# Stick-breaking attention from running products of sigmoid(-z), with differenced values shifted through DRAM

## The chip, the cores and the metric

The kernel runs on one core of a Trainium2 chip. The metric is the device time of one execution in microseconds (us); lower is better. The engines are named as in the profile: PE multiplies matrices (PEld loads its weights), DVE is the vector engine, ACT the scalar engine, POOL is GpSimd, and SP issues most of the loads.

## The reference, cut to what matters

One layer of an encoder on 1024 tokens of width 1024: two token mixers side by side (causal pooling and stick-breaking attention), gated, projected and added to the input; then an MLP with squared ReLU. The part that the change rewrites is the attention, eight heads of 64 channels:

```python
z = einsum('bhqd,bhkd->bhqk', qb, kb) * scale
mask = arange(t1)[None, :] < arange(t0, t1)[:, None]        # s < t
log_1mb = where(mask, log_sigmoid(-z), 0.0)
tail = cumsum(log_1mb, reverse=True) - log_1mb
attn = where(mask, exp(log_sigmoid(z) + tail), 0.0)
out = einsum('bhqk,bhkd->bhqd', attn, vb)
```

So A[t,s] = sigmoid(z[t,s]) times the product of sigmoid(-z[t,j]) over s < j < t. Write F[t,s] for the product of sigmoid(-z[t,j]) over s <= j < t. Then F[t,t] = 1 and A[t,s] = F[t,s+1] - F[t,s], since sigmoid(z) = 1 - sigmoid(-z).

## The kernel before

All activations are held transposed or in tiles of 128 tokens. Every float32 product of weights and activations is made as three matmuls in a reduced float32 format on high and low parts (`mm3`, L113 to L117). The kernel has four phases: `phase_in` (norm, pooling mixer, first q and k), `phase_attention`, `phase_post` (branch and output projections) and `phase_mlp`.

In `phase_attention` the rows of scores of one head go from row tile 7 to row tile 0. `att_scores` makes z in PSUM with two matmuls for each chunk of at most 512 columns (L561, L564), then two sigmoids on ACT: F = sigmoid(-z) (L565) and T = sigmoid(z) (L566). POOL sets T to zero at and above the diagonal of the last 128 columns (`affine_select`, L568), DVE turns F into a running product from right to left (`tensor_tensor_scan`, L574; its second operand `past` forces 1 where s >= t), and DVE multiplies T by F one column further right (L578). T is then A.

`att_steps` takes a group g of four row tiles: for each source tile s it transposes the four blocks of T on PE (L591), splits them into a high part on ACT (L599) and a low part on DVE (L600), and one step later `att_products` multiplies by the v tile of s into the PSUM tile `o` (L616). A v tile holds, for four heads, 64 columns of high and 64 of low parts, so `o` has two halves by partition; after the last s they are copied and added into `oT` (L625, L627). `o` has one buffer. When s is the group's last tile, POOL clears part of the high and low tiles first (L597, L598).

Between these steps PE gets dense work as filler: gate projections (`job_gate`, stored through POOL's queue at L521), the q and k of later heads (`job_qk`) and v (`job_v`). `pump` counts out how many steps of filler stand between two steps of attention; with `pin`, the first matmul of each three is issued behind a mark that lies four marks back (L111 to L113). v of heads 0 to 3 is made at the start of head 0, source tiles 7 to 0, and v of heads 4 to 7 inside heads 3 and 4, tiles 0 to 7. `job_v` evicts one tile of 128 tokens by 256 columns with one ACT instruction (L508) and one DVE instruction (L509).

The order within each engine's queue is not that of the program: a planner sets it when the kernel is built, from its own estimates of durations, and `issue_after` adds an edge that it has to keep. Each engine then runs its queue strictly in that order and waits on semaphores.

POOL's queue also issues `weight_sums` (L1067, L1069): 32 transfers from DRAM to DRAM that prepare sums of MLP weights, some of them accumulating. Before the change one of them is issued after the masking of every second row (L673 to L675), 28 in the attention phase.

Of the kernel before, what the change touches and what calls it, by code (L numbers as in the profile page):

```python
# [19 lines left out]
F32 = mybir.dt.float32  # L20
F32R = mybir.dt.float32r
BF16 = mybir.dt.bfloat16
AF = mybir.ActivationFunctionType
ALU = mybir.AluOpType
# [28 lines left out]
class Block:  # L53
# [53 lines left out]
    def mm3(self, ps, terms, first=True, last=True):  # L107
        nc = self.nc
        n = len(terms)
        for i, (wh, wl, rh, rl) in enumerate(terms):  # L110
            if self.pin and len(self.marks) >= LAG:  # L111
                with self.tc.issue_after(self.marks[-LAG].ins):
                    nc.tensor.matmul(ps, wh, rh, start=first and i == 0, stop=False)  # L113
            else:
                nc.tensor.matmul(ps, wh, rh, start=first and i == 0, stop=False)  # L115
            nc.tensor.matmul(ps, wh, rl, start=False, stop=False)  # L116
            nc.tensor.matmul(ps, wl, rh, start=False, stop=last and i == n - 1)  # L117

    def dense_steps(self, ps, wt, rhs, c0=0, cn=H):

# [51 lines left out]
    def build(self):  # L172
# [61 lines left out]
        self.rp = tc.alloc_tile_pool(name="row", bufs=1, side="left")  # L234
        self.rb = [self.rp.tile([P, H], F32, name=f"rb{h}") for h in range(2)]
        self.rcol = cp.tile([P, NK], F32, name="rcol")
        edge = tc.alloc_tile_pool(name="edge", bufs=1, side="right")
        self.edge = edge.tile([P, 24], F32, name="edge")
        self.dps = tc.alloc_tile_pool(name="att_d", bufs=2, space=PSUM)
# [11 lines left out]
    def phase_in(self):  # L251
# [46 lines left out]
            load(1, k, 2)  # L298
        for t, src in zip((self.eye, self.rcnt), self.consts):
            nc.sync.dma_start(t, src)  # L300
        past = pa.tile([P, 1024], F32, name="past")
        nc.gpsimd.memset(past, 1.0)
        nc.gpsimd.affine_select(
# [112 lines left out]
        def pool_mix(g, cur):  # L416
            sc = self.vt[:, V_PSC + g : V_PSC + g + 1]
            yl = us[g]
            ph = pb.tile([P, 1024], F32R, name="ph")
            pq = pb.tile([P, 1024], F32R, name="pq")  # L420
            nc.scalar.copy(ph, cur)
            nc.vector.tensor_sub(pq, cur, ph.bitcast(F32))
            for h in range(2):
                c = slice(h * H, h * H + H)
                d = self.zps.tile([P, H], F32, name="dm", tag=("o", "at")[h], bufs=h + 1)
                self.mm3(d, [(wmh[:, g, :], wml[:, g, :], ph[:, c], pq[:, c])])
                nc.scalar.activation(cur[:, c].bitcast(F32R), d, AF.Copy, scale=sc)
                nc.vector.scalar_tensor_tensor(
                    out=yl[:, c].bitcast(F32R), in0=d, scalar=sc, in1=cur[:, c], op0=ALU.mult, op1=ALU.subtract
                )  # L430
            for t, scr in zip((cur, yl), self.yscr[g]):
                nc.gpsimd.dma_start(scr.bitcast(F32), t)
# [18 lines left out]
        pool_mix(2, pooled[2])  # L451
        pooled.append(pool_group(3))
        self.run(self.job_qk("k", 0, 0))
        pool_mix(3, pooled[3])
        self.run(self.job_qk("k", 0, 1))
        pb.release()

    def run(self, gen):
# [30 lines left out]
    def job_v(self, grp):  # L489
        nc = self.nc  # L490
        w = [self.weights(("v", grp, j), 1 - j) for j in range(2)]

        for t in range(NK) if grp else range(NK - 1, -1, -1):
            d = self.dps.tile([P, H], F32, name="dv", tag="d")
            h, c = t // 4, (t % 4) * P
            rh, rl = self.hT[h]
            for k in range(NK):
                wh, wl = w[k // 4]
                b = slice((k % 4) * 256, (k % 4) * 256 + 256)
                self.mm3(  # L500
                    d[:, :256], [(rh[:, k, c : c + P], rl[:, k, c : c + P], wh[:, b], wl[:, b])], k == 0, k == NK - 1
                )
                if k % 2:
                    yield
            v = self.vp.tile([P, 4, P], F32R, name=f"v{grp}_{t}", tag="v", bufs=9)
            dd = d[:, :256].rearrange("p (h x) -> p h x", h=4)
            r = self.rcol[:, t : t + 1]
            nc.scalar.activation(v[:, :, 0:64], dd, AF.Copy, scale=r)  # L508
            nc.vector.scalar_tensor_tensor(  # L509
                out=v[:, :, 64:128], in0=dd, scalar=r, in1=v[:, :, 0:64].bitcast(F32), op0=ALU.mult, op1=ALU.subtract  # L510
            )
            self.v[(grp, t)] = v

    def job_gate(self, i, h):
        nc = self.nc
# [22 lines left out]
    def att_scores(self, h, i):  # L538

        nc = self.nc
        p, j = h // 2, h % 2
        q, qs, k = self.qk[("q", p)][j], self.qk[("qs", p)][j], self.qk[("k", p)][j]
        w = (i + 1) * P
        tl = self.tp.tile([P, w], F32, name="T", tag=f"T{i}", bufs=1)
        f = self.tp.tile([P, 1024], F32, name="F", tag="F", bufs=1)
        tt = slice(i * P, i * P + P)  # L550
        past = self.past[:, 1024 - w :]

        low = min(H, w - 2 * P) if w > H else 0
        for c, n in ((low, w - low), (0, low)):
            if n == 0:
                continue
            top = c == low
            cols = slice(c, c + max(256, n))
            z = self.zps.tile([P, H], F32, name="z", tag="z", bufs=3)
            zz = z[:, : max(256, n)]  # L560
            m = nc.tensor.matmul(zz, q[:, tt], k[:, cols], start=True, stop=False)  # L561
            if top:
                self.marks.append(m)
            nc.tensor.matmul(zz, qs[:, tt], k[:, cols], start=False, stop=True)  # L564
            nc.scalar.activation(f[:, c : c + n], z[:, :n], AF.Sigmoid, scale=-1.0)  # L565
            nc.scalar.activation(tl[:, c : c + n], z[:, :n], AF.Sigmoid)  # L566
            if top:
                self.masked = nc.gpsimd.affine_select(  # L568
                    out=tl[:, w - P : w], in_=tl[:, w - P : w], pattern=[[-1, P]], compare_op=ALU.is_gt, fill=0.0,
                    base=0, channel_multiplier=1,  # L570
                )

            fr = f[:, c : c + n][:, ::-1]
            nc.vector.tensor_tensor_scan(  # L574
                fr, fr, past[:, c : c + n][:, ::-1], 1.0 if top else f[:, c + n : c + n + 1], ALU.mult, ALU.max
            )
            e = c + n - top
            nc.vector.tensor_mul(tl[:, c:e], tl[:, c:e], f[:, c + 1 : e + 1])  # L578
        return tl

    def att_steps(self, h, g, a):
# [3 lines left out]
        for s in range(4 * g + 4):  # L585
# [9 lines left out]
            c0, c = min(r0, 2) * P, r0 * P  # L595
            if r0 == 3:
                nc.gpsimd.memset(hi[:, c0:c].bitcast(F32), 0.0)  # L597
                nc.gpsimd.memset(lo[:, c0:c].bitcast(F32), 0.0)  # L598
            nc.scalar.copy(hi[:, c:], at[:, c:])  # L599
            nc.vector.tensor_sub(lo[:, c:], at[:, c:], hi[:, c:].bitcast(F32))  # L600
            self.att_products()
            self.pending = (h, g, s, o, hi, lo, c0)
            yield

    def att_products(self):
# [14 lines left out]
        if not last:  # L620
            return
        b = 64 * (h % 2)
        for c in (0, 256):
            u = self.sp.tile([P, 256], F32, name="ou", tag="ou", bufs=1)
            nc.scalar.copy(u[64:128, :], o[64:128, c : c + 256])  # L625
            at = slice(g * H + c, g * H + c + 256)
            nc.vector.tensor_add(self.oT[h // 2][b : b + 64, at], o[0:64, c : c + 256], u[64:128, :])  # L627

    def pump(self, share):
        self.credit += share  # L630
# [14 lines left out]

    def phase_attention(self):
        tc, nc = self.tc, self.nc
        self.oT = [self.op.tile([P, 1024], F32, name=f"oT{p}", tag=f"oT{p}") for p in range(4)]
        kw = dict(side="right", reuse_waits="tile")
        self.tp = tc.alloc_tile_pool(name="att", bufs=1, **kw)  # L650
        self.sp = tc.alloc_tile_pool(name="att_s", bufs=1, **kw)
# [6 lines left out]
        for h in range(8):  # L658
# [4 lines left out]
            self.queue = fl  # L663
            share = [WS[i] for i in ROWS] if h else [0.0] * 4 + [WS[i] for i in ROWS[4:]]
            w_in = max(0.0, n - (8 if h == 0 else 12) * self.w_out) / sum(share)
            vg = self.job_v(0) if h == 0 else None
            a = {}
            for n_row, i in enumerate(ROWS):
                if n_row == 4:
                    out = self.att_steps(h, 1, [a[r] for r in range(4, 8)])  # L670
                a[i] = self.att_scores(h, i)
                self.pump(w_in * share[n_row])
                if h < 7 and n_row % 2:  # L673
                    with tc.issue_after(self.masked.ins):
                        next(self.wsums)  # L675
                if h == 0 and n_row < 4:
                    if n_row == 0:
                        vq = [(vg, 32)] + [(f[0], f[1]) for f in self.fillers(-1)]
                    left = 12 if n_row < 3 else 999
                    while vq and left:  # L680
                        left -= 1
                        if next(vq[0][0], self) is self:
                            vq.pop(0)
                if out is not None:
                    for _ in range(2 if n_row > 3 else 1):
                        next(out, None)
# [705 lines left out]
```

## Time and profile before

| | us |
|---|---|
| median of 3 runs | 1275.92 |
| lowest, highest run | 1275.71, 1277.13 |
| span of the profiled execution | 1274.1 |

The span goes from the first to the last instruction of one profiled execution; the page gives no other time of that execution. The median of the runs is 1.8 us above it. Busy shares of an engine are shares of that span; "idle before" in a group of instructions is the time in which that engine stood just before them, followed by the line that ended it.

### The profile page before, as it was taken

What the parts mean: (1) busy time and instruction counts of PE and PEld (TensorE: products, weight loads), DVE (VectorE), ACT (ScalarE), POOL (GpSimd) and SP (SyncE); (2) the same over time, 40 slices, a digit from 0 to 9 for tenths busy, and PEclk for the clock granted to TensorE, in tenths of its full rate; (3) what the DMA queues carried; (4) which work ended last, traced back from release to release, by engine and by line L of the source; (5) the groups of instructions that cost most, each with busy time, mean ns of one, the idle gap of its engine ahead of it and who ended that gap; (6) DMA issues with size and microseconds to landing.
All of it is one profiled execution on the core that took longest, in us unless ns stands there. A gap on an engine that the chain in (4) does not pass through costs nothing.

```text
span 1274.1 us, 16614 instructions
## 1 busy us (share of the span) xinstructions
PE 1266.1 (99%) x6043; PEld 1057.7 (83%) x6043; DVE 924.9 (73%) x1315; ACT 614.6 (48%) x1022; POOL 169.6 (13%) x314
## 2 busy tenths in 40 slices
PE   9999999999999999999999999999999999999998
PEld 6898888889888888888878888888888888888887
DVE  8787688786878747551777988877775655776975
ACT  8235455564555542232456646455454433344452
POOL 1002213221223121100101002212120000001000
PEclk9999999999999999999999999999999999999999
DMA  6254447694686138671529578656559546556551
GB/s 226 67 165 166 146 161 163 138 219 141 124 215 223 67 120 232 198 219 33 182 85 303 183 247 277 219 198 208 199 205 346 193 154 223 189 179 238 199 220 67
DMA packets 75729, 233.70 MB, mean 183 GB/s; under 512 B 8608, under 2 KB 11168, under 8 KB 73472
## 3 DMA queue, kind: packets, MB, share of 16 engines
q1 hardware_dynamic: 48352, 144.04, 33.9%
q0 software_dynamic: 27152, 88.49, 23.7%
q8 instruction: 47, 0.77, 0.2%
q14 instruction: 34, 0.28, 0.1%
q10 hardware_dynamic: 144, 0.13, 0.0%
HBM read 178.10 MB, written 83.89 MB: 206 GB/s over the span
## 4 chain that ended last, share of the span: by engine, by line
PE 94%; DVE 3%; issue 1%; ACT 1%; DMA 1%; POOL 0%; SPq 0%; DVEq 0%; ACTq 0%; POOLq 0%
PE d L116 20%; PE d L117 20%; PE d L115 20%; PE dg L117 4%; PE dg L116 4%; PE dg L113 4%; PE o L616 3%; PE at L591 2%; PE dqk L116 2%; PE dqk L117 2%; PE dqk L113 1%; PE z L564 1%; PE z L561 1%; DVE F L574 1%; PE dv L117 1%
## 5 line engine op out<-in xcount | busy, mean ns | idle before, releaser
L116 PE MATMUL d<-blo,whi 128*128 128x512 f32 (+1 forms) x456 | 172.3, 378 | 0.0
L117 PE MATMUL d<-bhi,wlo 128*128 128x512 f32 (+1 forms) x456 | 171.9, 378 | 0.0
L115 PE MATMUL d<-bhi,whi 128*128 128x512 f32 (+1 forms) x456 | 168.7, 378 | 0.0
L574 DVE TENSOR_TENSOR_SCAN F<-F,past 128x256 f32<-128x256 f32 (+2 forms) x96 | 94.2, 981 | 20.9 <-ACT F L565 20.0
L85 ACT CAST whi<-wraw 128x512 fp32r<-128x512 f32 (+1 forms) x88 | 67.7, 799 | 77.2 <-PE d L116 38.0
L113 PE MATMUL dg<-hT_hi,whi 128*128 128x512 f32 x253 | 101.7, 402 | 0.0
L117 PE MATMUL dg<-hT_hi,wlo 128*128 128x512 f32 x256 | 100.8, 394 | 0.0
L116 PE MATMUL dg<-hT_lo,whi 128*128 128x512 f32 x256 | 100.4, 392 | 0.0
L117 PEld LDWEIGHTS d<-bhi,wlo 128*128 128x128 f32 x456 | 85.8, 188 | 15.9
L116 PEld LDWEIGHTS d<-blo,whi 128*128 128x128 f32 x456 | 85.7, 188 | 15.9
L115 PEld LDWEIGHTS d<-bhi,whi 128*128 128x128 f32 x456 | 85.5, 188 | 16.1
L86 DVE TENSOR_TENSOR wlo<-wraw,whi 128x512 fp32r<-128x512 f32 (+1 forms) x88 | 77.7, 905 | 28.4 <-ACT whi L85 28.3
L116 PE MATMUL d<-b_lo,whi 128*128 128x512 f32 x196 | 76.2, 390 | 0.4 <-DVE b_lo L836 0.4
L115 PE MATMUL d<-b_hi,whi 128*128 128x512 f32 x196 | 75.6, 389 | 0.0
L565 ACT ACTIVATE F<-z 128x256 f32<-128x256 f32 (+2 forms) x96 | 47.2, 493 | 58.8 <-DVE T L578 34.4
L117 PE MATMUL d<-b_hi,wlo 128*128 128x512 f32 x196 | 74.7, 389 | 0.0
L1124 DVE TENSOR_TENSOR wlo<-slots_hi,whi 128x1024 fp32r<-128x1024 f32 x29 | 35.5, 1225 | 53.1 <-ACT whi L1122 53.1
L600 DVE TENSOR_TENSOR alo<-at,ahi 128x512 fp32r<-128x512 f32 (+1 forms) x96 | 52.0, 553 | 29.9 <-ACT ahi L599 28.8
L1122 ACT CAST whi<-slots_hi 128x1024 fp32r<-128x1024 f32 x29 | 30.5, 1052 | 84.5 <-PE d L116 71.5
L599 ACT CAST ahi<-at 128x512 fp32r<-128x512 f32 (+1 forms) x96 | 45.1, 482 | 47.4 <-PE at L591 44.0
L1122 ACT CAST whi<-slots_lo 128x1024 fp32r<-128x1024 f32 x27 | 28.4, 1053 | 73.4 <-PE d L116 59.7
L578 DVE TENSOR_TENSOR T<-T,F 128x255 f32<-128x255 f32 (+3 forms) x96 | 53.1, 556 | 11.0 <-POOL T L568 2.5
(323 smaller groups left out, 3309.3 us busy)
## 6 DMA issues: line engine op xcount, KB each, us to landing
wraw<-w SPq DMA_DIRECT2D x80, 512.0 KB, 4.3
wscr<-w POOLq DMA_DIRECT2D x24, 1024.0 KB, 10.0
ext_b<-ascr SPq DMA_DIRECT2D x40, 512.0 KB, 4.3
gscr<-gs POOLq DMA_DIRECT2D x32, 256.0 KB, 4.2
gate<-gscr POOLq DMA_DIRECT2D x16, 512.0 KB, 4.5
pscr<-p SPq DMA_DIRECT2D x32, 256.0 KB, 3.2
braw<-w SPq DMA_DIRECT2D x16, 512.0 KB, 5.1
ascr<-c POOLq DMA_DIRECT2D x32, 256.0 KB, 5.0
```

Of the source, the lines that this page charges most:

```text
L85: nc.scalar.copy(hi[:, c], raw[:, c])
L86: self.last_lo = nc.vector.tensor_sub(lo[:, c], raw[:, c], hi[:, c].bitcast(F32)).ins
L113: nc.tensor.matmul(ps, wh, rh, start=first and i == 0, stop=False)
L115: nc.tensor.matmul(ps, wh, rh, start=first and i == 0, stop=False)
L116: nc.tensor.matmul(ps, wh, rl, start=False, stop=False)
L117: nc.tensor.matmul(ps, wl, rh, start=False, stop=last and i == n - 1)
L565: nc.scalar.activation(f[:, c : c + n], z[:, :n], AF.Sigmoid, scale=-1.0)
L574: nc.vector.tensor_tensor_scan(fr, fr, past[:, c : c + n][:, ::-1], 1.0 if top else f[:, c + n : c + n + 1], ALU.mult, ALU.max)
L578: nc.vector.tensor_mul(tl[:, c:e], tl[:, c:e], f[:, c + 1 : e + 1])
L599: nc.scalar.copy(hi[:, c:], at[:, c:])
L600: nc.vector.tensor_sub(lo[:, c:], at[:, c:], hi[:, c:].bitcast(F32))
L1122: last_split[0] = nc.scalar.copy(hi, src).ins
```

## The change: what it does

The difference A[t,s] = F[t,s+1] - F[t,s] is moved from the attention weights to the values. With v[-1] = 0 the output is the sum over the row tile's columns s of F[t,s] (v[s-1] - v[s]), plus v at the last token of the row tile; columns s >= t, where F is 1, telescope away.

In `att_scores` the second sigmoid, the POOL mask and the DVE multiplication are gone, as is the tile F; sigmoid(-z) and its running product are written straight into T. In `job_v` the evicted v tile goes to DRAM (`vscr`, one row further down, row 0 is zero) and comes back twice, once one row earlier; DVE takes the difference and it is split into high and low parts. The loads are two tiles behind the stores and the splits one more (three at the end of the job). Four small loads for each job bring the last row of each row tile into `vlast`, transposed, and the eviction of `o` adds it as a bias. Row 0 of the output is set to zero. The order of the work around head 0 is changed, and the weight sums go out two at a time behind the clearing at the end of each group.

```diff
     def mm3(...)
+            self.last_mm = nc.tensor.matmul(ps, wl, rh, start=False, stop=last and i == n - 1).ins
     def build(self):
+        self.vlast = cp.tile([P, 8, NK], F32, name="vlast")
+        self.vscr = dp.tile([1 + P * NK, H], F32, name="vscr")
     def phase_in(self):
+        nc.gpsimd.memset(self.pad, 0.0)
+        nc.gpsimd.dma_start(self.vscr[0:1, :].rearrange("o (p n) -> (o p) n", p=P), self.pad[:, 0:4])
...
+                with self.tc.issue_after(self.last_mm) if g == 3 else contextlib.nullcontext():
+                    self.mm3(d, [(wmh[:, g, :], wml[:, g, :], ph[:, c], pq[:, c])])
...
         self.run(self.job_qk("k", 0, 0))
+        self.run(self.job_qk("k", 0, 1))
+        self.vg0 = self.job_v(0)
+        for _ in range(12):
+            next(self.vg0)
         pool_mix(3, pooled[3])
-        self.run(self.job_qk("k", 0, 1))
     def job_v(self, grp):
+        room = self.op.tile([P, 2, 2, 256], F32, name=f"vroom{grp}", tag=f"oT{1 + 2 * grp}")
+        def load(t):
+            b = room[:, len(pairs) % 2]
+            for j in range(2):
+                nc.gpsimd.dma_start(b[:, j, :], self.vscr[t * P + j : t * P + j + P, cols])
+            pairs[t] = b
+        def split(t):
+            b = pairs[t]
+            e = b[:, 0, :]
+            nc.vector.tensor_sub(e, e, b[:, 1, :])
+            e = e.rearrange("p (h x) -> p h x", h=4)
+            v = self.vp.tile([P, 4, P], F32R, name=f"v{grp}_{t}", tag="v", bufs=9)
+            nc.scalar.copy(v[:, :, 0:64], e)
+            nc.vector.tensor_sub(v[:, :, 64:128], e, v[:, :, 0:64].bitcast(F32))
...
-            nc.scalar.activation(v[:, :, 0:64], dd, AF.Copy, scale=r)
-            nc.vector.scalar_tensor_tensor(out=v[:, :, 64:128], ...)
+            s = self.sp.tile([P, 256], F32, name="vs", tag="vs", bufs=3)
+            nc.scalar.activation(s, d[:, :256], AF.Copy, scale=self.rcol[:, t : t + 1])
+            nc.gpsimd.dma_start(self.vscr[1 + t * P : 1 + t * P + P, cols], s)
+            behind.append(t)
+            if len(behind) > 2:
+                load(behind[-3])
+            if len(behind) > 3:
+                split(behind[-4])
+        for t in behind[-2:]:
+            split(behind[behind.index(t) - 1])
+            load(t)
+        split(behind[-1])
+        for h in range(4 * grp, 4 * grp + 4):
+            nc.gpsimd.dma_start(self.vlast[64:128, h, :], self.vscr[P : P * NK + 1 : P, 64 * h : 64 * h + 64].rearrange("i d -> d i"))
     def att_scores(self, h, i):
+            with self.tc.issue_after(self.last_mm) if h == 0 and i > 3 else contextlib.nullcontext():
+                m = nc.tensor.matmul(zz, q[:, tt], k[:, cols], start=True, stop=False)
-            nc.scalar.activation(f[:, c : c + n], z[:, :n], AF.Sigmoid, scale=-1.0)
-            nc.scalar.activation(tl[:, c : c + n], z[:, :n], AF.Sigmoid)
-            if top:
-                self.masked = nc.gpsimd.affine_select(out=tl[:, w - P : w], ...)
+            f = tl[:, c : c + n]
+            nc.scalar.activation(f, z[:, :n], AF.Sigmoid, scale=-1.0)
             nc.vector.tensor_tensor_scan(...)
-            nc.vector.tensor_mul(tl[:, c:e], tl[:, c:e], f[:, c + 1 : e + 1])
     def att_steps(self, h, g, a):
+            if s == 4 * g + 3 and h < 7:
+                with self.tc.issue_after(self.zeroed.ins):
+                    next(self.wsums)
+                    next(self.wsums)
     def att_products(self):
-            nc.scalar.copy(u[64:128, :], o[64:128, c : c + 256])
+            for j in (0, P):
+                i = (g * H + c + j) // P
+                nc.scalar.activation(u[64:128, j : j + P], o[64:128, c + j : c + j + P], AF.Identity, bias=self.vlast[64:128, h, i : i + 1])
...
+        if g == 0:
+            nc.gpsimd.memset(self.oT[h // 2][b : b + 64, 0:1], 0.0)
     def phase_attention(self):
-                a[i] = self.att_scores(h, i)
-                self.pump(w_in * share[n_row])
-                if h < 7 and n_row % 2:
-                    with tc.issue_after(self.masked.ins):
-                        next(self.wsums)
                 if h == 0 and n_row < 4:
-                    left = 12 if n_row < 3 else 999
+                    left = 10 if n_row < 3 else 999
...
+                a[i] = self.att_scores(h, i)
+                self.pump(w_in * share[n_row])
```

In head 0 the filler of a row now stands ahead of that row's scores, not behind them. The tiles of `oT` are made when they are first needed, because `room` uses the place of two of them.

More of the change, by code (lines that the diff above doesn't have):

```diff
@@ L116, in mm3 @@
             nc.tensor.matmul(ps, wh, rl, start=False, stop=False)
-            nc.tensor.matmul(ps, wl, rh, start=False, stop=last and i == n - 1)
+            self.last_mm = nc.tensor.matmul(ps, wl, rh, start=False, stop=last and i == n - 1).ins
     def dense_steps(self, ps, wt, rhs, c0=0, cn=H):
@@ L425, in pool_mix @@
                 d = self.zps.tile([P, H], F32, name="dm", tag=("o", "at")[h], bufs=h + 1)
-                self.mm3(d, [(wmh[:, g, :], wml[:, g, :], ph[:, c], pq[:, c])])
+                with self.tc.issue_after(self.last_mm) if g == 3 else contextlib.nullcontext():
+                    self.mm3(d, [(wmh[:, g, :], wml[:, g, :], ph[:, c], pq[:, c])])
                 nc.scalar.activation(cur[:, c].bitcast(F32R), d, AF.Copy, scale=sc)
@@ L491, in job_v @@
         w = [self.weights(("v", grp, j), 1 - j) for j in range(2)]
+        cols = slice(256 * grp, 256 * grp + 256)
+        behind, pairs = [], {}
+        room = self.op.tile([P, 2, 2, 256], F32, name=f"vroom{grp}", tag=f"oT{1 + 2 * grp}")
[12 more added lines that the diff above has]
+            nc.vector.tensor_sub(v[:, :, 64:128], e, v[:, :, 0:64].bitcast(F32))
+            self.v[(grp, t)] = v
         for t in range(NK) if grp else range(NK - 1, -1, -1):
@@ L504, in job_v @@
                     yield
[L505 to L510, printed above, removed]
+            s = self.sp.tile([P, 256], F32, name="vs", tag="vs", bufs=3)
[11 more added lines that the diff above has]
+        for h in range(4 * grp, 4 * grp + 4):
+            nc.gpsimd.dma_start(
+                self.vlast[64:128, h, :], self.vscr[P : P * NK + 1 : P, 64 * h : 64 * h + 64].rearrange("i d -> d i")
             )
-            self.v[(grp, t)] = v
     def job_gate(self, i, h):
@@ L548, in att_scores @@
         tl = self.tp.tile([P, w], F32, name="T", tag=f"T{i}", bufs=1)
-        f = self.tp.tile([P, 1024], F32, name="F", tag="F", bufs=1)
         tt = slice(i * P, i * P + P)
@@ L560, in att_scores @@
             zz = z[:, : max(256, n)]
-            m = nc.tensor.matmul(zz, q[:, tt], k[:, cols], start=True, stop=False)
+            with self.tc.issue_after(self.last_mm) if h == 0 and i > 3 else contextlib.nullcontext():
+                m = nc.tensor.matmul(zz, q[:, tt], k[:, cols], start=True, stop=False)
             if top:
@@ L564, in att_scores @@
             nc.tensor.matmul(zz, qs[:, tt], k[:, cols], start=False, stop=True)
-            nc.scalar.activation(f[:, c : c + n], z[:, :n], AF.Sigmoid, scale=-1.0)
-            nc.scalar.activation(tl[:, c : c + n], z[:, :n], AF.Sigmoid)
-            if top:
[L568 to L573, printed above, removed]
+            f = tl[:, c : c + n]
+            nc.scalar.activation(f, z[:, :n], AF.Sigmoid, scale=-1.0)
             nc.vector.tensor_tensor_scan(
-                fr, fr, past[:, c : c + n][:, ::-1], 1.0 if top else f[:, c + n : c + n + 1], ALU.mult, ALU.max
-            )
-            e = c + n - top
-            nc.vector.tensor_mul(tl[:, c:e], tl[:, c:e], f[:, c + 1 : e + 1])
+                f[:, ::-1], f[:, ::-1], past[:, c : c + n][:, ::-1], 1.0 if top else tl[:, c + n : c + n + 1],
+                ALU.mult, ALU.max,
+            )
         return tl
@@ L597, in att_steps @@
                 nc.gpsimd.memset(hi[:, c0:c].bitcast(F32), 0.0)
-                nc.gpsimd.memset(lo[:, c0:c].bitcast(F32), 0.0)
+                self.zeroed = nc.gpsimd.memset(lo[:, c0:c].bitcast(F32), 0.0)
             nc.scalar.copy(hi[:, c:], at[:, c:])
@@ L622, in att_products @@
         b = 64 * (h % 2)
+        if h // 2 not in self.oT:
+            self.oT[h // 2] = self.op.tile([P, 1024], F32, name=f"oT{h // 2}", tag=f"oT{h // 2}")
         for c in (0, 256):
             u = self.sp.tile([P, 256], F32, name="ou", tag="ou", bufs=1)
-            nc.scalar.copy(u[64:128, :], o[64:128, c : c + 256])
+            for j in (0, P):
+                i = (g * H + c + j) // P
+                nc.scalar.activation(
+                    u[64:128, j : j + P], o[64:128, c + j : c + j + P], AF.Identity, bias=self.vlast[64:128, h, i : i + 1]
+                )
             at = slice(g * H + c, g * H + c + 256)
             nc.vector.tensor_add(self.oT[h // 2][b : b + 64, at], o[0:64, c : c + 256], u[64:128, :])
+        if g == 0:
+            nc.gpsimd.memset(self.oT[h // 2][b : b + 64, 0:1], 0.0)
     def pump(self, share):
@@ L647, in phase_attention @@
         tc, nc = self.tc, self.nc
-        self.oT = [self.op.tile([P, 1024], F32, name=f"oT{p}", tag=f"oT{p}") for p in range(4)]
+        self.oT = {}
         kw = dict(side="right", reuse_waits="tile")
@@ L665, in phase_attention @@
             w_in = max(0.0, n - (8 if h == 0 else 12) * self.w_out) / sum(share)
-            vg = self.job_v(0) if h == 0 else None
+            vg = self.vg0 if h == 0 else None
             a = {}
```

## The prediction

> **What bounds the kernel now.** I read the page first, then what PE waited for, then the attention stage in stretches of 64 us, then single matmuls in order of time.
>
> ```profile
> span 1274.1 us, 16614 instructions
> ...
> PE 1266.1 (99%) x6043; PEld 1057.7 (83%) x6043; DVE 924.9 (73%) x1315; ACT 614.6 (48%) x1022; POOL 169.6 (13%) x314
> ...
> PE 94%; DVE 3%; issue 1%; ACT 1%; DMA 1%; POOL 0%; SPq 0%; DVEq 0%; ACTq 0%; POOLq 0%
> ```
>
> PE stands still for 1274.1 - 1266.1 = 8.0 us of the whole span, and the chain that ended last is 94% PE. A busy PE need not be PE at its peak, so the stage has to be looked at more closely. Windows (length, then busy time and count of PE, PEld, DVE, ACT, POOL, granted clock, DMA share, GB/s):
>
> ```profile
> 64.00:128.00 64.00, 63.62 (x382) 56.56 (x381) 50.55 (x80) 31.46 (x58) 9.83 (x17) 1.00 0.49 165
> 128.00:192.00 64.00, 64.00 (x319) 53.31 (x318) 46.80 (x74) 32.59 (x70) 13.72 (x26) 1.00 0.47 155
> 192.00:256.00 64.00, 64.00 (x323) 53.70 (x322) 53.30 (x83) 36.98 (x82) 17.43 (x32) 1.00 0.73 151
> 256.00:320.00 64.00, 63.63 (x414) 57.60 (x413) 49.01 (x83) 35.39 (x79) 12.42 (x24) 1.00 0.66 175
> 320.00:384.00 64.00, 64.00 (x322) 53.69 (x321) 52.23 (x81) 36.60 (x79) 16.59 (x31) 1.00 0.74 173
> 384.00:448.00 64.00, 63.59 (x323) 53.32 (x322) 50.79 (x82) 36.56 (x80) 14.94 (x31) 1.00 0.41 142
> ...
> 512.00:576.00 64.00, 64.00 (x284) 53.01 (x283) 36.80 (x48) 17.75 (x24) 5.93 (x9) 1.00 0.70 201
> ```
>
> Attention lies in the first six. PE is short of its 64 us by 0.38, 0.37 and 0.41 us in three of them, **1.16 us** in all. The last window is dense projection with nothing else: 284 matmuls of 512 columns in 64 us, 225 ns each. Inside attention the same spacing holds:
>
> ```profile
> 125.00 0.40 PE L117 MATMUL dg<-hT_hi,wlo 128*128 128x512 f32 x1
> 125.23 0.40 PE L113 MATMUL dg<-hT_hi,whi 128*128 128x512 f32 x1
> 125.47 0.39 PE L116 MATMUL dg<-hT_lo,whi 128*128 128x512 f32 x1
> ```
>
> The starts are 230 and 240 ns apart (rounded), so no waits hide in the durations of 0.4 us. What PE waited for (times in us, count, longest):
>
> ```profile
> PE at L591 <- DVE T L578: 0.4, 1, 0.4
> ...
> PE dg L115 <- DVE v L509: 0.4, 1, 0.4
> PE o L616 <- DVE oT L627: 0.4, 1, 0.4
> ```
>
> These three are the 1.16 us. All end with DVE. DVE is busy for 50 of 64 us and ACT for 35, but PE's filler covers them. So the stage is bound by how many matmuls there are.
>
> The Trainium skill ("Perfetto Trace Analysis", Identifying the Most-Contended Engine) warns of just this reading: matmul busy time is no good measure, weight-load time is better. By PEld there would be room, as it fills 53 of 64 us. The trace disagrees here: the dense window has the same 53.01 us of PEld with matmuls at an even 225 ns, so 83% is what a full PE looks like in this kernel.
>
> **The change part by part.** Groups, with count, busy us, mean ns, idle before:
>
> ```profile
> L566 ACT ACTIVATE T<-z 128x256 f32<-128x256 f32 (+2 forms) x96 | 47.0, 493 | 0.0
> L578 DVE TENSOR_TENSOR T<-T,F 128x255 f32<-128x255 f32 (+3 forms) x96 | 53.1, 556 | 11.0 <-POOL T L568 2.5 <-ACT T L566 1.4
> L568 POOL TENSOR_SCALAR_AFFINE_SELECT T<-T 128x128 f32<-128x128 f32 x64 | 34.8, 544 | 168.9 <-ACT T L566 156.8 <-PE o L616 6.4 <-PE dqk L117 5.6
> L508 ACT ACTIVATE v<-dv,rcol 128x256 fp32r<-128x256 f32 x16 | 7.7, 479 | 12.3 <-PE dv L117 12.1
> L509 DVE SCALAR_TENSOR_TENSOR v<-dv,rcol,v 128x256 fp32r<-128x256 f32 x16 | 7.6, 477 | 3.8 <-ACT v L508 3.8
> L625 ACT COPY ou<-o 64x256 f32<-64x256 f32 x32 | 11.8, 368 | 13.0 <-PE o L616 8.5 <-DVE oT L627 3.9
> L599 ACT CAST ahi<-at 128x128 fp32r<-128x128 f32 x16 | 4.3, 270 | 4.8 <-PE at L591 4.7
> ```
>
> *PE*: the same matmuls for z, transposes, v and o, of the same shapes. Change 0. This is the term that decides.
>
> *Scores*: ACT loses 47.0 us, DVE 53.1, POOL 34.8. All of it lies beside PE, so it is worth at most the 1.16 us of stalls that end with DVE. The chain from z to a finished T loses a sigmoid, the mask and the product. Writing F into T's place makes the first sigmoid wait for the last head's transposes of that tile; the second sigmoid waited for them already. Cost 0.
>
> *Values*: for each of 16 tiles ACT keeps one instruction like L508 and gets a second, 16 x 0.48 = 7.7 us; DVE gets one more, 16 x 0.48 = 7.6. *Eviction of o*: 32 copies of 368 ns become 64 of 128 columns; at the 270 ns of the nearest row (128 columns, 128 partitions) that is 17.3 us for 11.8, about 0.17 us more in each half before `o` is free. Net, ACT falls by 34 us and DVE by 45, again beside PE. `o` is late once in 16 groups now (0.4 us); 0.34 us more on ACT against shorter queues on both engines is worth between -0.4 and +16 x 0.34 = 5.4; I take 0, since DVE, which releases PE there, loses most.
>
> *DMAs on POOL's queue*: 16 stores, 32 loads and 8 gathers of `vlast` are added. POOL's rows, and two issue lines with KB and us to landing:
>
> ```profile
> L521 POOL DMA_DIRECT2D gscr<-gs x32 | 18.8, 587 | 84.5 <-ACT gs L520 56.7 <-ACT ahi L599 23.5 <-PE dqk L117 4.1
> ...
> gscr<-gs POOLq DMA_DIRECT2D x32, 256.0 KB, 4.2
> ...
> wraw<-w POOLq DMA_DIRECT2D x3, 128.0 KB, 4.8
> ...
> DMA to landing us min/median/max: 2.3/4.4/11.3
> ```
>
> The 48 cost POOL 48 x 0.59 = 28 us, less than the 34.8 that go. A store lands after some 4.2 us, a load of the same size as here after 4.8; the last row (all uses of `gscr`) shows the spread. The new wait: a load waits on POOL for its stores to land, and behind it on POOL stand later stores, gate stores, the clearing and the weight sums. After the last v matmul of a job the chain is: ACT 0.5, store and two load issues 1.8, landing 4.8, split 3 x 0.48 = 1.4, which frees a half of `room`; then two issues 1.2, landing 4.8, split 1.4. Sum **15.9 us**, where it was 1.0 (L508, L509). What covers it:
>
> ```profile
> 105.43 0.28 PE L117 MATMUL dv<-whi,hT_lo 128*128 128x256 f32 x1
> ...
> 127.43 0.40 PE L616 MATMUL o<-ahi,v 128*128 128x512 f32 x1
> ...
> 274.25 0.28 PE L113 MATMUL dv<-whi,hT_hi 128*128 128x256 f32 x1
> ...
> 304.56 0.28 PE L117 MATMUL dv<-whi,hT_lo 128*128 128x256 f32 x1
> ...
> 325.62 0.28 PE L616 MATMUL o<-ahi,v 128*128 128x256 f32 x1
> ```
>
> In head 0 the last v matmul is at 105.4 and the first use of v tile 0, the tile made last, at 127.4: 22 us of gates and scores. In the second job tile 7 is made last at 304.6 and used at 325.6: 21 us. So 5 to 6 us are left over, and the cost on PE is 0; without that cover it would be up to 15 us in each job.
>
> The `vlast` gathers have no row like them. Four-byte pieces, 512 for each, cost POOL at least the 0.59 us of an issue; if an issue grows with the rows (128 there), 2.4. They are needed at the end of a group, over 10 us later. I take 0 on PE. The Trainium skill ("DMA: Bandwidth & Descriptors", Rules for kernel authors) says that a transfer whose last dimension isn't contiguous becomes one descriptor per element, which speaks against them; no row here shows it.
>
> *Moved steps*: `job_qk` and 12 steps of v ahead of the pooling mix change only the order. The stall at 106.3 belongs to that place:
>
> ```profile
> 97.77 2.91 DMA yscr<-win
> ...
> 103.20 0.78 POOL T L568
> 104.01 0.69 DVE T L578
> 104.70 1.20 DVE F L574
> 105.89 0.39 DVE v L509
> 106.32 0.50 PE dg L115
> ```
>
> T needs the room of `win`, whose store goes out on POOL; then came the table, the mask, the product and the scan. Mask and product (1.47 us) leave the chain, but the store may now stand behind a load that waits up to 4.2 us. Between -0.4 and +3; I take -0.4, since the first v tiles are evicted long before. Weight sums in pairs: same bytes, two at once behind the clearing; a weight load beside them lands later but is needed a job (16 steps of 3 matmuls, 11 us) on. 0.
>
> *Sum*: 1274.1 - 1.16 for the stalls + 0.4 for one new one of their usual size = 1273.3 in the profiled execution. The median of runs stands 1.8 above its span: **1275.2 us**, 0.06% down. A measurement of this kernel tells about 0.2% (2.6 us) from no change.
>
> **The rivals.** *The waiting splits stop DVE and ACT* (slower). The splits stand in strict queues with the running products and the low parts that PE needs. In the second job a v tile takes (304.6 - 274.3) / 8 = 3.8 us; a load needs 0.6 + 4.8 = 5.4 after its first issue, so a split put where the program has it stands 1.6 us, about the 2.3 steps of filler (2.3 x 3 x 0.225 = 1.55) between a transpose and its product: no loss. The two splits at the end that directly follow their loads stand 5.4 us each, 3.9 over the cover: 7.7 us, 1282.9. It decides if the planner thinks loads much quicker than 5 us. For it: nothing else stands between them in the program. Against: in the trace PE waits only 1.16 us although weight loads also land 4 us late, so the planner's times are fair. Chance 0.16.
>
> *v comes late to head 0* (slower). If two landings in a row take 8 to 11 us, as the slowest of `gscr`, the chain is 22 to 28 us against 22: 0 to 6, I price 4: 1279.2. Against: the weight sums, the big transfers, now leave that stretch. Chance 0.11.
>
> *The stage isn't bound by PE after all* (faster). Were PEld the measure, 10 of 64 us could go; by the even spacing none. With a few us in all, 1271. Chance 0.04.
>
> *It does nothing on the path*: the forecast itself, 0.69.
>
> **How the numbers follow.** Forecast 0.69, its own range 1274.5 to 1277.5 (all stalls gone; two or three more of 0.4 to 1 us). The range goes on to the late v and to half of the stopped DVE: 1274.2 to 1280.8. Faster by over 0.2% 0.04, within 0.69, slower 0.27.
>
> **What would show it.** Right: 6043 matmuls on PE, PE idle within 1 us of 8.0, DVE and ACT lower by some 45 and 34 us, POOL waits of several us at loads of `room`, first use of v some 20 us after its last matmul. Wrong: PE idle before `o` at the first step of head 0 (late v), before transposes or products near the end of a v job with DVE waiting on a DMA (stopped splits), before the first `o` of many groups (eviction); or fewer than 225 ns per matmul (PE not bound).

## The result and the profile after

| | us, kernel before | us, changed kernel |
|---|---|---|
| median of 4 runs | 1276.53 | 1291.78 |
| lowest, highest | 1275.71, 1277.57 | 1289.88, 1293.26 |
| span of the profiled execution | 1274.1 | 1291.6 |

The changed kernel is slower: ratio 1.012, interval 1.0105 to 1.0134, about 15 us. The forecast was no change (1275.2, range to 1280.8). One execution of e6 below (3778 us) and one of e9 (3300 us) stand far above all others of the same kernel and are left out of their medians. The page of the changed kernel first:

```profile
span 1291.6 us, 16464 instructions
...
PE 1274.1 (99%) x6043; PEld 1062.7 (82%) x6043; DVE 882.3 (68%) x1234; ACT 592.0 (46%) x973; POOL 168.3 (13%) x316
```

The work fell as meant: DVE by 43 us, ACT by 23, and PE still has 6043 matmuls. But PE now stands still for 1291.6 - 1274.1 = 17.5 us, where it was 8.0, and the same matmuls count as 8.0 us more of busy time. Some 2 us of the difference lie at the very start: 60 matmuls run in the first 20 us where it was 68, with a granted clock of 0.88 and 0.95 in the two halves of that stretch and 1.00 before. That varies from run to run, as e6 to e8 show. What PE waited for (times in us, count, longest):

```profile
PE dg L113 <- ACT vs L534: 2.8, 1, 2.8
PE dv L113 <- ACT vs L534: 1.9, 2, 1.0
PE dv L115 <- ACT vs L534: 1.8, 2, 1.1
PE dm L115 <- ACT ph L425: 1.7, 1, 1.7
...
PE dm L116 <- DVE pq L426: 0.8, 1, 0.8
```

The three waits that the kernel before had in attention are gone. In their place PE waits, in attention, for the eviction of v into its staging tile `vs` (L534), 6.5 us, and for the last pooling mix, 2.5 us. Windows of the changed kernel (columns as before) show where:

```profile
64.00:128.00 64.00, 59.75 (x346) 52.77 (x346) 43.92 (x71) 27.00 (x50) 20.50 (x37) 0.95 0.52 169
...
256.00:320.00 64.00, 62.12 (x403) 56.06 (x402) 39.45 (x62) 30.53 (x69) 17.13 (x30) 1.00 0.78 166
320.00:384.00 64.00, 60.86 (x288) 49.77 (x287) 41.95 (x69) 30.14 (x66) 14.75 (x31) 0.95 0.61 194
```

Two places, and both are v jobs: 92 to 110 us (first job) and 301 to 332 us (second). In two windows the granted clock is 0.95 as well. Single matmuls of the second place show both halves of the price:

```profile
322.32 0.39 PE L116 MATMUL dg<-hT_lo,whi 128*128 128x512 f32 x1
322.54 0.39 PE L117 MATMUL dg<-hT_hi,wlo 128*128 128x512 f32 x1
325.78 0.80 PE L113 MATMUL dg<-hT_hi,whi 128*128 128x512 f32 x1 [2.85 <-ACT vs L534]
326.37 0.63 PE L116 MATMUL dg<-hT_lo,whi 128*128 128x512 f32 x1
326.80 0.63 PE L117 MATMUL dg<-hT_hi,wlo 128*128 128x512 f32 x1
327.23 0.63 PE L113 MATMUL dg<-hT_hi,whi 128*128 128x512 f32 x1
```

Starts are 0.22 us apart before the gap and 0.43 behind it. This goes on to 332 us: 14 matmuls, with some 0.2 us too much for each of 512 columns and 0.1 for each of 256, 3 us on top of the wait. The Trainium skill ("TensorE: Matmul & The Clock Gate", Part 1: The HAM clock gate) states that PE falls to half its clock after about 3.4 us of idleness and gives 426.7 ns for 512 columns then. The 0.43 us here agree; the gap, 3.2 us between the starts at 322.54 and 325.78, is a little shorter than that.

The first place has half rate too, and there no such gap stands ahead of it:

```profile
92.27 0.28 PE L117 MATMUL dv<-whi,hT_lo 128*128 128x256 f32 x1
94.21 0.50 PE L115 MATMUL dm<-ph,wmh 128*128 128x512 f32 x1 [1.66 <-ACT ph L425]
95.47 0.50 PE L116 MATMUL dm<-pq,wmh 128*128 128x512 f32 x1 [0.76 <-DVE pq L426]
...
96.53 0.63 PE L117 MATMUL dm<-ph,wml 128*128 128x512 f32 x1
98.30 0.58 PE L115 MATMUL dv<-whi,hT_hi 128*128 128x256 f32 x1 [1.14 <-ACT vs L534]
98.68 0.42 PE L116 MATMUL dv<-wlo,hT_hi 128*128 128x256 f32 x1
98.89 0.41 PE L117 MATMUL dv<-whi,hT_lo 128*128 128x256 f32 x1
```

From here to 103.2 us the matmuls of 256 columns start 0.21 us apart, where 0.12 is usual: some 2 us. No two starts from 92.27 us on lie 2 us apart. In e2 the same place, with waits of 1.58, 0.76 and 1.14 us, keeps the full rate (granted clock 1.00 in the window), and in e1 a wait of 3.26 us is followed by only some 2.5 us at half rate. So half rate added between 0 and 3 us to a stall in these runs, and what decides how much is not shown.

**The second place.** POOL's queue, then ACT's, in order of time:

```profile
307.90 2.43 POOL L1104 DMA_DIRECT2D wscr<-w  x2
309.21 1.71 POOL L535 DMA_DIRECT2D vscr<-vs  x1
309.80 2.21 POOL L508 DMA_DIRECT2D vroom<-vscr  x2
310.88 2.19 POOL L535 DMA_DIRECT2D vscr<-vs  x2
...
325.46 1.08 POOL L508 DMA_DIRECT2D vroom<-vscr  x2 [11.61 <-DMA vscr<-vs]
```

```profile
302.25 0.47 ACT L534 ACTIVATE vs<-dv,rcol 128x256 f32<-128x256 f32 x1 [4.90 <-DMA vscr<-vs]
...
325.25 0.47 ACT L534 ACTIVATE vs<-dv,rcol 128x256 f32<-128x256 f32 x1 [9.19 <-DMA vscr<-vs]
```

Two weight sums of 1 MB go out at 307.9 and three stores of v, with two loads between them, right behind. The stores land only at 325, so all three staging tiles are out. ACT stands 9.19 us at the next eviction with everything else behind it; that eviction would free a PSUM bank, PE uses up the other one and stops. The same happened behind the pair before it (issued at 285.5): 4.90 us. All transfers of `vs` in this stretch:

```profile
DMA to landing us min/median/max: 2.2/13.0/16.0
```

The six stores behind a pair of sums took 8.4 to 16.0 us, the other two 2.2 and 2.3.

**The first place.** ACT's queue:

```profile
96.23 0.69 ACT L432 ACTIVATE win<-dm,vt 128x512 fp32r<-128x512 f32 x1 [2.07 <-PE dm L117]
97.19 0.69 ACT L432 ACTIVATE win<-dm,vt 128x512 fp32r<-128x512 f32 x1 [0.27 <-PE dm L117]
97.78 0.83 ACT L534 ACTIVATE vs<-dv,rcol 128x256 f32<-128x256 f32 x2
```

No sum is near. Two v tiles are evicted only at 97.8, behind ACT's last instruction of the pooling mix, though ACT had stood idle for 2.07 us. They hold both PSUM banks, so PE has no filler while it waits for the mix's inputs, and then waits for the banks.

### The profile page after: what moved, and what is told of

Same layout as the page of the kernel before. It is cut to its first block, busy times and chain, and to the rows that moved or that the text cites. A ratio compares the mean times of both kernels' runs of the same rounds, so it can differ in the third digit from the quotient of the medians.

```text
span 1291.6 us, 16464 instructions
## 1 busy us (share of the span) xinstructions
PE 1274.1 (99%) x6043; PEld 1062.7 (82%) x6043; DVE 882.3 (68%) x1234; ACT 592.0 (46%) x973; POOL 168.3 (13%) x316
## 5 line engine op out<-in xcount | busy, mean ns | idle before, releaser
L603 DVE TENSOR_TENSOR_SCAN T<-T,past 128x256 f32<-128x256 f32 (+2 forms) x96 | 93.3, 975 | 31.2 <-ACT T L602 28.1
L113 PE MATMUL dg<-hT_hi,whi 128*128 128x512 f32 x240 | 96.8, 403 | 2.8 <-ACT vs L534 2.8
L117 PEld LDWEIGHTS d<-bhi,wlo 128*128 128x128 f32 x456 | 85.8, 188 | 15.9
L602 ACT ACTIVATE T<-z 128x256 f32<-128x256 f32 (+2 forms) x96 | 45.2, 492 | 45.1 <-PE z L600 44.3
L1161 DVE TENSOR_TENSOR wlo<-slots_lo,whi 128x1024 fp32r<-128x1024 f32 x27 | 33.0, 1223 | 35.7 <-ACT whi L1159 35.6
```

The lines of the kernel that those rows point to most:

```text
L117: self.last_mm = nc.tensor.matmul(ps, wl, rh, start=False, stop=last and i == n - 1).ins
L602: nc.scalar.activation(f, z[:, :n], AF.Sigmoid, scale=-1.0)
L603: nc.vector.tensor_tensor_scan(f[:, ::-1], f[:, ::-1], past[:, c : c + n][:, ::-1], 1.0 if top else tl[:, c + n : c + n + 1], ALU.mult, AL ...
L1161: last_split[1] = nc.vector.tensor_sub(lo, src, hi.bitcast(F32)).ins
```

## The experiments

Ratios are against the kernel before on the same chip. Line numbers of the kernels move by up to 7.

**e4: the change without the trip.**

```diff
 job_v:
-            s = self.sp.tile([P, 256], F32, name="vs", tag="vs", bufs=3)
...
+            nc.scalar.activation(v[:, :, 0:64], dd, AF.Copy, scale=r)
+            nc.vector.scalar_tensor_tensor(out=v[:, :, 64:128], in0=dd, scalar=r, ...)
 att_products:
-                nc.scalar.activation(u[...], o[...], AF.Identity, bias=self.vlast[...])
+            nc.scalar.copy(u[64:128, :], o[64:128, c : c + 256])
```

> Leaves out the difference of the values, the trip through DRAM and the bias; v is split straight from PSUM as before, the rest (short chain of scores, order of head 0, paired sums) is that of the changed kernel, so the attention output lacks the shift. Theory A (the 15 us are all due to the trip; the shorter scores give nothing since PE is full): 1274 to 1277. Rival (the new order in head 0 and the pins cost by themselves): 1280 or more, with PE still dry at 92 to 99 us.

1276.55 us against 1276.29, ratio 1.0002 (0.9992 to 1.0011). PE waits for nothing in attention. The shorter scores, the new order of head 0 and its pins cost and gain nothing that can be measured, and neither do the paired sums here; the loss comes only with the trip.

**e1: the staging tiles in another place.**

```diff
-            s = self.sp.tile([P, 256], F32, name="vs", tag="vs", bufs=3)
+            s = self.vp.tile([P, 256], F32, name="vs", tag="vs", bufs=3)
```

> Only the place of the three staging tiles vs is changed: they come from the pool of the v tiles, which lives through both phases, not from a pool that is laid over the pooling mix's memory. Theory A (place): tiles 5 and 4 of the first v job are evicted late (97.8 us) because their staging tiles lie where the pooling mix still works; both PSUM banks of dv stay full and PE runs dry at 92 to 99 us. Then the stalls at 92 to 110 us (7 us against before) go, the one at 300 to 340 us stays: 1284 to 1286. Rival (order): the eviction of tile 5 is written behind the last pooling mix in the program and stays behind it on ACT: no change, 1291.

1283.64 us, ratio 1.0052 (1.0036 to 1.0069): 8.1 us less than the changed kernel (between the two sets of runs the kernel before differs by 0.2 us). ACT's queue and the first of the three windows in e1:

```profile
90.48 0.47 ACT L534 ACTIVATE vs<-dv,rcol 128x256 f32<-128x256 f32 x1 [0.62 <-PE dv L117]
93.41 0.48 ACT L534 ACTIVATE vs<-dv,rcol 128x256 f32<-128x256 f32 x1 [2.45 <-PE dv L117]
...
96.29 0.48 ACT L534 ACTIVATE vs<-dv,rcol 128x256 f32<-128x256 f32 x1 [1.16 <-issue]
```

```profile
64.00:128.00 64.00, 64.00 (x385) 57.06 (x384) 48.61 (x77) 30.57 (x56) 21.17 (x39) 1.00 0.58 182
```

With the program otherwise the same, the third eviction comes 7.3 us earlier and the fourth 4.7, and PE is full. So it was the place: from the third tile on, `vs` comes from a pool that is laid over the pooling mix's memory. Which of the mix's tiles they had to wait for isn't told apart. The second place is as before (PE waits 3.3 us at its worst gate matmul).

**e2: no weight sum while the second v job runs.**

```diff
 job_v, from its start to its end:
+        self.v_open = True
...
+        self.v_open = False
 att_steps:
             if s == 4 * g + 3 and h < 7:
-                with self.tc.issue_after(self.zeroed.ins):
-                    next(self.wsums)
-                    next(self.wsums)
+                if self.v_open:
+                    self.owed += 2
+                else:
+                    with self.tc.issue_after(self.zeroed.ins):
+                        for _ in range(2 + min(1, self.owed)):
+                            next(self.wsums)
+                    self.owed -= min(1, self.owed)
```

> Only the weight sums move: none goes out while the second v job runs (heads 3 and 4), later groups send three until the four are made up. Theory A (sums): in the second job the stores of v stand behind two sums of 1 MB and land after 8 to 16 us; with three staging tiles ACT then stands 4.9 and 9.2 us and PE 0.9, 1.0 and 2.8 us, and PE runs at half clock for a while behind it. Then stores land in 2 to 5 us and some 8 us go: about 1283. Rival (the wait itself): POOL's own waits for stores and loads are enough to stop ACT: no change beyond 2 us, 1289 to 1291.

1282.99 us, ratio 1.0052 (1.0037 to 1.0067): 8.8 us less. All transfers of `vs` in the second job, and the windows of the second place:

```profile
DMA to landing us min/median/max: 2.0/2.2/2.8
```

```profile
256.00:320.00 64.00, 64.00 (x415) 58.21 (x414) 46.12 (x76) 34.86 (x79) 19.71 (x39) 1.00 0.54 145
320.00:384.00 64.00, 64.00 (x322) 53.51 (x322) 42.30 (x65) 31.17 (x67) 13.59 (x24) 1.00 0.86 226
```

The median landing falls from 13.0 to 2.2 us and PE is full in both windows. Who waited for `vs` in this job, in the changed kernel and in e2 (us, times):

```profile
POOL vroom L508: 20.6, 3
...
POOL vroom L510: 3.8, 2
```

POOL still stands ahead of loads until stores have landed, but no longer for long, and ACT does not stand for staging tiles at all. The rival had no change, so it falls. The first place is still there (PE busy 58.91 us of its 64).

**e5: both cures at once.**

> Both cures at once: the staging tiles in their own place (as in e1) and no weight sum while the second v job runs (as in e2). Theory A (two separate causes, 8 us each, that add up): both stretches clean, no PE wait for vs; 1275.5 to 1277.5, that is the same as before, with the start of the kernel still 1 to 2 us late. Rival (one cause shows twice, or the trip has a further price): 1280 or more.

1276.15 us, ratio 0.9998 (0.9989 to 1.0007). The two prices, 8.1 and 8.8 us, 16.9 together, make up the 15.6 us between the changed kernel and e5 within the scatter of the medians.

```profile
PE 1267.1 (99%) x6043; PEld 1059.7 (83%) x6043; DVE 881.3 (69%) x1234; ACT 592.1 (46%) x973; POOL 168.5 (13%) x316
```

With a span of 1274.4 us PE is idle for 7.3 us. The trip itself, with all its waits on POOL, then costs nothing, and the 43 us less on DVE gain nothing.

**e6 and e7: the first transfer.** e6 is e5 with the zero row of `vscr` written some 60 us later, e7 is the kernel before with that early transfer added:

```diff
 e6, phase_in (from before the memset of past to here):
+        nc.gpsimd.memset(self.pad, 0.0)
+        nc.gpsimd.dma_start(self.vscr[0:1, :].rearrange("o (p n) -> (o p) n", p=P), self.pad[:, 0:4])
         for h in range(2):
             columns(h)
 e7, build and phase_in of the kernel before:
+        self.vscr = dp.tile([1 + P * NK, H], F32, name="vscr")
...
+        nc.gpsimd.memset(self.pad, 0.0)
+        nc.gpsimd.dma_start(self.vscr[0:1, :].rearrange("o (p n) -> (o p) n", p=P), self.pad[:, 0:4])
         past = pa.tile([P, 1024], F32, name="past")
```

> e5, and the first transfer on POOL's queue (the zero row of vscr, 128 pieces of 16 bytes at 4 us) is issued some 60 us later. In the changed kernel and e1 to e4 the first 20 us take 1.4 to 2.3 us more than in the one profile of before. Theory A (that transfer delays the first loads): the first 20 us are as before and the time falls by 1 to 2 us against e5: 1274 to 1276. Rival (the start varies from run to run): no change against e5.

> The kernel before with only that first transfer and its memset added at the place where the changed kernel has it. Theory A: 1 to 2 us slower than before, all of it in the first 20 us. Rival (run to run): no change.

e6: 1275.54 us, ratio 0.9993 (0.9984 to 1.0002). e7: 1277.15 us, ratio 1.0003 (0.9994 to 1.0012). Neither can be told from the kernel before. In the profiled executions e7, with the early transfer, has a granted clock of 1.00 in the first 20 us and runs 65 matmuls there; e8 below, without it, has 0.94 and 0.89 in the two halves and runs 59. So the late start does not come from that transfer; it varies from run to run. e6 is the fastest version of the change, but not shown to be faster than the kernel before.

**e8: pairs of sums without the trip.** The kernel before, with the sums issued as in the changed kernel:

```diff
-                if h < 7 and n_row % 2:
-                    with tc.issue_after(self.masked.ins):
-                        next(self.wsums)
...
 att_steps:
+            if s == 4 * g + 3 and h < 7:
+                with self.tc.issue_after(self.zeroed.ins):
+                    next(self.wsums)
+                    next(self.wsums)
```

> The kernel before with the weight sums sent two at a time behind the clearing at each group's end, as in the changed kernel; v is made without the trip. Theory A (pairs harm only because v's stores and loads stand behind them): same as before within 0.2%, 1275 to 1278. Rival (pairs also hold up weight loads and gate stores that PE needs): 1279 or more.

1276.43 us, ratio 0.9999 (0.9990 to 1.0008). Pairs as such are free. They cost only with the trip behind them.

**e10: one sum instead of two while the second job runs.**

```diff
-                    next(self.wsums)
-                    next(self.wsums)
+                n = 1 if self.v_open else 2 + min(1, self.owed)
+                self.owed += 2 - n
...
+                    for _ in range(n):
+                        next(self.wsums)
```

> The changed kernel, with one weight sum instead of two at each group's end while the second v job runs, the rest made up later. Theory A (stores stand behind the sums' packets, each 1 MB about 5 us): they land after 5 to 10 us instead of 8 to 16, ACT stands for less than half, 2 to 6 us of the 8 that the sums cost go: 1285 to 1289. Rival (any sum there is enough to fill the staging tiles): 1290 to 1292.

1286.08 us, ratio 1.0077 (1.006 to 1.0094): 5.7 us less than with two, 3.1 more than with none (e2). The transfers of `vs` in that stretch lie between the two as well:

```profile
DMA to landing us min/median/max: 2.1/4.6/9.2
```

**e3: the stores from ACT's queue.**

```diff
-            nc.gpsimd.dma_start(self.vscr[1 + t * P : 1 + t * P + P, cols], s)
+            nc.scalar.dma_start(self.vscr[1 + t * P : 1 + t * P + P, cols], s)
```

> Only the 16 stores of v go out from ACT's queue, not POOL's; the loads and the sums stay. Theory A (the queue): a store behind the sums on POOL's queue waits for their packets; on another queue it lands in 2 to 5 us, ACT doesn't stand for staging tiles, the stall at 300 to 340 us goes: about 1283, and the one at 92 to 110 us stays or falls a little. Rival (the engines): the 16 DMA engines are full of the sums whatever the queue, the stores still take 8 us and more: 1289 to 1292.

1295.20 us, ratio 1.0148 (1.0133 to 1.0163): no cure, and above the rival's range as well, for another reason than either gave. The transfers of `vs` in the second job, then DVE's queue:

```profile
DMA to landing us min/median/max: 1.9/6.6/7.4
```

```profile
325.59 0.43 DVE L514 TENSOR_TENSOR vroom<-vroom 128x256 f32<-128x256 f32 x1 [9.05 <-DMA vroom<-vscr]
326.05 0.42 DVE L665 TENSOR_TENSOR oT<-o,ou 64x256 f32<-64x256 f32 x1
```

The stores land in 6.6 instead of 13.0 us, where e2 has 2.2. So both theories had a part: of 10.8 us of delay 6.4 went with the queue, and 4.4 stayed. That these are due to the shared DMA engines is the rival's account; no run tests it alone. ACT no longer stands for `vs`. But the loads still go out on POOL behind the sums. DVE stops 9.05 us at a split that waits for one, and behind the split stands the addition that frees `o`; PE waits 5.3 us for it. The Trainium skill ("DMA: Bandwidth & Descriptors", Queues, rings and completion order) says that each DMA engine takes turns between the queues that have work and takes the descriptors of one queue in order; by that rule a store on its own queue passes the sums but shares their engines, and the 6.6 us fit it.

**e9: a fourth staging tile**, on top of e1:

```diff
-            s = self.vp.tile([P, 256], F32, name="vs", tag="vs", bufs=3)
+            s = self.vp.tile([P, 256], F32, name="vs", tag="vs", bufs=4)
```

> e1 with four staging tiles vs instead of three; sums as in the changed kernel. Theory A (ACT stands because all staging tiles are out in stores that land after 8 to 16 us): a fourth tile gives ACT one v tile more (3.8 us) before it has to stand, so of the stands of some 5 and 9 us in the second job some 5 us in all are left, and of e1's 7 us over the kernel before 2 to 4 remain: 1278.5 to 1281. Rival (loads and splits behind the sums stop DVE, as in e3, whatever the staging): 1283 to 1285, as e1.

1284.80 us, ratio 1.0065 (1.0048 to 1.0081): no gain over e1, against my expectation and as the rival had it. ACT and DVE in its second job:

```profile
316.82 0.41 ACT L517 CAST v<-vroom 128x256 fp32r<-128x256 f32 x1 [7.85 <-DVE vroom L514]
```

```profile
316.36 0.43 DVE L514 TENSOR_TENSOR vroom<-vroom 128x256 f32<-128x256 f32 x1 [8.80 <-DMA vroom<-vscr]
```

ACT doesn't stand for `vs` here, but DVE and ACT stand nearly as long at the next step of the trip, the split, whose load waits for the same late stores, and PE waits 4.5 us for a high part that stands behind it on ACT. The staging tiles were only where the delay showed first. The cause is the trip behind the sums on one queue.

## Why the prediction was wrong

**PE is full, so what DVE and ACT lose is worth nothing: right.** e4 and e5 are within 0.1% of the kernel before. The three stalls went too, worth the 1.16 us at most that the sum gave them.

**"Weight sums in pairs: same bytes, ... 0": the first step that failed**, about 8 us (e2). It asked who else needs the DMA engines and named the weight loads, which indeed don't matter (e8). It did not ask what the change itself puts behind the sums on the same queue. The landing times of 4.2 and 4.8 us, one of which stands twice in the 15.9 us of the chain, are medians of other transfers on that queue: the stores of the trip take 2.2 us with no sum ahead of them and 8.4 to 16.0 behind two. The row of the spread (2.3/4.4/11.3) was shown, and its 11.3 was charged to head 0, where no sum was left, instead of to the second job, where two pairs go out (at 285.5 and 307.9).

**"Between -0.4 and +3; I take -0.4, since the first v tiles are evicted long before": the second**, about 8 us (e1). Two of the first four tiles are evicted after the mix, because their staging tiles lie over its memory. The working followed the store of `win` through POOL's queue, but not where the new tiles come from. A new buffer is a new wait, and it holds a PSUM bank for as long.

**The sum left out the clock.** Behind the gap at 322.5 us the matmuls run at half rate for some 6 us, 3 us more; at the first place half rate adds some 2.

**The rivals.** That waiting splits stop DVE and ACT had a chance of 0.16 and a price of 7.7 us for the second job. The mechanism is the one that e3 and e9 show, with 9.05 and 8.80 us on DVE, and the price is close to the 8.8 us of e2. But what set it off was the sums in front of the load, which the rival did not name; it had the last two splits of the job stand 5.4 us each for a load with nothing in front. That the prices are close is luck. In the changed kernel itself ACT's wait for staging tiles came first. v coming late to head 0 did not happen: no PE wait is for v.

**Sizes that were off without an effect.** An eviction of `o` takes 357 ns, not 270, so the 64 take 19.8 us and not 17.3. ACT loses 23 us on the page where the sum had 34; the eviction explains 2.5 us of these 11, and the rest was not taken apart (records of ACT overlap, so groups add up to more than the page's busy time). It costs nothing:

```profile
L661 ACT ACTIVATE ou<-o,vlast 64x128 f32<-64x128 f32 x64 | 19.8, 357 | 16.2 <-PE o L648 13.3 <-DVE oT L665 2.4
```

The 15.9 us leave out a landing. In the first job the load of tile 1 needs a row of tile 0, so it waits for the last store too, 4.5 us. The last v matmul of that job is at 113.8 us, its last split ends at 132.8, 19 us later, and the first use is at 139.8, so the cover held. The upper end of the range, 1280.8, does not follow from the terms named for it: the late v gives 1279.2 and half of the stopped DVE 1279.1.

## What to carry to other kernels

Before costing a transfer by its usual landing time, look at what its own queue holds ahead of it: large transfers that nobody waits for are free until something short with a waiter is put behind them. A trip through DRAM adds a buffer at each end, and each is a wait in a strict queue: ask where the buffer lies, who used that place last, and what stands behind the instruction that needs it. Where PE is full, taking 43 us from another engine buys nothing, and the only open question of such a change is what new wait it makes.

## What the runs showed of the hardware

A store of 128 KB that lands in 2.2 us (median) with no sum ahead of it takes up to 16.0 us behind two accumulating transfers of 1 MB on the same queue, and 6.6 us (median, at most 7.4) from another queue beside them. Half rate of PE came behind a wait of 2.85 us, but also with no two starts 2 us apart, and in another run the same short waits left the clock at 1.00. The gathers of `vlast`, 512 pieces of 4 bytes each, were cheap:

```profile
L546 POOL DMA_DIRECT2D vlast<-vscr x8: 707/716/732, 121.6 to 332.1; - x8
...
DMA to landing us min/median/max: 2.5/2.7/3.8
```

They take POOL 0.72 us to issue and land after 2.7, little more than the plain loads of 128 rows into `vroom` (0.54 and 2.5).
